# A block's maximum and its scaling in one instruction: products with minus the scale, their minimum accumulated

## The chip, the core and the metric

The kernel runs on one NeuronCore of a Trainium2 chip. The core has five engines with a queue each: TensorE (PE, matmuls), VectorE (DVE), ScalarE (ACT), GpSimd (POOL) and SyncE (SP, which here issues DMAs). Each works through its own queue in order and waits on semaphores for the others. The metric is the device time of one execution, in microseconds (us).

## What is computed

One layer of a streaming encoder on 512 tokens of width 1024 in float32: a modulated RMS norm and one input projection, then a convolution branch and an attention branch side by side, an output projection with a residual, and a mixture of experts. The change touches the attention alone, 8 heads, queries in blocks of 128:

```python
def block_attn(args):
    qb, blk = args
    sc = jnp.einsum("bqhd,bkhd->bhqk", qb, k).astype(jnp.float32) * scale
    q_chunk = (blk * Q_BLOCK + jnp.arange(Q_BLOCK)) // CHUNK
    mask = key_chunk[None, :] <= q_chunk[:, None]
    sc = jnp.where(mask[None, None], sc, -jnp.inf)
    p = jax.nn.softmax(sc, axis=-1).astype(v.dtype)
    return jnp.einsum("bhqk,bkhd->bqhd", p, v)
```

## The kernel before

The program is one long sequence, laid out by hand: in the stretch at issue PE, DVE, ACT and POOL each execute in the order in which the code names them (`manual_schedule`), so an instruction that waits holds up all that stands behind it on its engine.

*Before the attention,* `qkv_mm` makes queries, keys and values for one tile of 128 tokens at a time. Queries are not normalised; the norm's factor per token and head is kept in `qs` (128 tokens x 4 tiles x 8 heads), a root taken on POOL (`root`, L193) from the sums of squares. `qs_due` holds this root back: it is issued in the next tile's `qkv_mm`, behind the root of the keys, and at once for the last tile.

*The attention* is a loop over 32 blocks (L926): 8 heads with 4 query tiles each, head by head. Block i has 128 queries and (i mod 4 + 1) x 128 keys, so 128 to 512 columns. `scores` forms the products on PE in a PSUM bank (L867; the mask is in four further rows of queries and keys, a large negative number), DVE takes the maximum over the columns (L868) and multiplies it by minus the scale (L869, one column), and ACT computes exp(scale x product + bias) into an SBUF tile `e` with that bias and accumulates the row sums (L871). Two blocks later `p_tr` transposes `e` on PE (L881) and copies it out of PSUM, on DVE for the two narrow query tiles, on ACT for the wide ones (L882). After every two heads `attn_out` spreads the reciprocal sums by 16 matmuls (L891), multiplies by the values (L899) and DVE scales the result (L905), which ACT and POOL split in two parts (L670, L675).

*Beside it* run the convolution's matmuls (L334) and its layer norm (`conv_norm`: L693 on DVE, squares on ACT, sums on PE at L697), and `split_wout`: from block 7 on, a piece of the output weights is copied in a reduced format on DVE (the cast, L829) and the remainder is formed on POOL (the subtraction, L831), 12 pieces of 128x512 over the blocks 7 to 20, with each fifth block left free.

The tiles `e` come from a pool of 7 buffers of 128x512 (`T()`), the PSUM banks of the scores from one of 4 (`acc`), those of the transposes from one of 2 (`tr`).

Of the kernel before, what the change touches and what calls it, by code (L numbers as in the profile page):

```python
# [17 lines left out]
OP = mybir.AluOpType  # L18
AX = mybir.AxisListType
# [22 lines left out]
def hybrid_block(ctx: ExitStack, tc: tile.TileContext, A, out, dbg=None, stop=None):  # L42
    nc = tc.nc
    pe, act, dve, pool, sp = nc.tensor, nc.scalar, nc.vector, nc.gpsimd, nc.sync
# [42 lines left out]
    def nm(s):  # L87
        uid[0] += 1
        return f"{s}_{uid[0]}"
# [4 lines left out]
    def S(shape, dt=F32):  # L94
        return slots.tile(shape, dt, tag="s", name=nm("s"))

    def T(shape=(128, 512), dt=F32):
        return tmp.tile(list(shape), dt, tag="t", name=nm("t"))

    def small(w, dt=F32, bufs=4, tag=None):  # L100
        return tmp.tile([128, w], dt, tag=tag or f"sm{w}", name=nm("sm"), bufs=bufs)

    def acc(shape=(128, 512), dt=F32):
        return psum.tile(list(shape), dt, tag="acc", name=nm("acc"), bufs=4)
# [7 lines left out]
    def C(shape, dt=F32, name=None, uname=None):  # L112
        return const.tile(list(shape), dt, tag=name, name=uname or name)

    def mm3(o, lh, ll, rh, rl, start, stop):
        pe.matmul(o, lh, rh, start=start, stop=False)  # L116
        pe.matmul(o, lh, rl, start=False, stop=False)  # L117
        pe.matmul(o, ll, rh, start=False, stop=stop)  # L118
# [68 lines left out]
    def mean_eps(ssq, n, scale, eps=EPS):  # L187
        t = small(n, tag=f"rs{n}")
        dve.tensor_scalar(t, ssq, float(scale), eps, op0=OP.mult, op1=OP.add)
        return t  # L190

    def root(o, t, n):
        return pool.tensor_tensor(o, t, nhalf[:, :n], op=OP.pow)  # L193
# [84 lines left out]
    def run(g, n=100):  # L278
        for _ in range(n):
            if next(g, 0) == 0:  # L280
                break
# [69 lines left out]
    def tap(n):  # L351
        q = taps
        while n and q:
            if next(q[0], 0) == 0:
                q.pop(0)
            else:
                n -= 1
                if len(q) > 1:
                    q[0], q[1] = q[1], q[0]
# [156 lines left out]
    for tt in range(4):  # L516
        p = pcc[tt]
# [5 lines left out]
    for tt in range(4):  # L523
        p = pcc[tt]
# [7 lines left out]
    def rope_apply(o, src, TA, TB, nh):  # L532

        s4 = src.rearrange("p h (i d) -> p h i d", i=2)
        o4 = o.rearrange("p h (i d) -> p h i d", i=2)
        m = T()
        a1 = m[:, :nh * 32].rearrange("p (h i d) -> p h i d", h=nh, i=2)
        a2 = m[:, 256:256 + nh * 32].rearrange("p (h i d) -> p h i d", h=nh, i=2)
        pool.tensor_tensor(a1, s4, TA, op=OP.mult)
        for i in range(2):  # L540
            pool.tensor_tensor(a2[:, :, i, :], s4[:, :, 1 - i, :], TB[:, :, i, :], op=OP.mult)
        pool.tensor_tensor(o4, a1, a2, op=OP.add)
# [178 lines left out]

    ks = C([128, 4, 8], name="ks")
    qs = C([128, 4, 8], name="qs")
    vt = S([128, 4, 512])
    qT = [S([128, 4, 512]) for _ in range(2)]
    kT = [S([128, 4, 512]) for _ in range(2)]
# [14 lines left out]
    def qkv_mm(tt, g):  # L741
        cc = slice(tt * 128, (tt + 1) * 128)
        qktok = S([128, 2, 8, 96])
        qtok, ktok = qktok[:, 0], qktok[:, 1]
        pk = acc()
        wv = wkvs.rearrange("p s (h z d) -> p s h z d", z=2, d=64)
        mm3(pk, cTh[:, 2, cc], cTl[:, 2, cc], wv[:, 0, :, 0, :], wv[:, 1, :, 0, :], True, True)
        pk3 = pk.rearrange("p (h d) -> p h d", d=64)
        sq = T()
        act.activation(sq, pk, AF.Square)  # L750
        ssk = small(8, tag="ssk")
        tap(TK if tt < 3 else T3[0])
        dve.tensor_reduce(ssk, sq.rearrange("p (h d) -> p h d", d=64), axis=AX.X, op=OP.add)
        dve.tensor_scalar(ssk, ssk, cst[:, tt, 2:3], None, op0=OP.add)
        mk = mean_eps(ssk, 8, 1.0 / 96)
        ssq = small(8, tag="ssq")
        for hh in range(2):
            p = acc()
            for c in range(2):
                ns = slice(384 * hh, 384 * hh + 384)  # L760
                mm3(p[:, :384], cTh[:, c, cc], cTl[:, c, cc], wqh[:, c, ns], wql[:, c, ns], c == 0, c == 1)
            pq = p[:, :384].rearrange("p (h d) -> p h d", d=96)
            act.copy(qtok[:, 4 * hh:4 * hh + 4, :], pq)
            sq = T()
            act.activation(sq[:, :384], p[:, :384], AF.Square)
            run(g, 1)
            tap(TQ if tt < 3 else T3[1])
            dve.tensor_reduce(ssq[:, 4 * hh:4 * hh + 4], sq[:, :384].rearrange("p (h d) -> p h d", d=96), axis=AX.X, op=OP.add)
        rope_apply(qtok[:, :, 64:], qtok[:, :, 64:], *(t_[:, tt, None].to_broadcast([128, 8, 2, 16]) for t_ in rope["q"]), 8)
        root(ks[:, tt, :], mk, 8)  # L770
        for f in qs_due:
            f()
        qs_due.clear()
        dve.tensor_tensor(ktok[:, :, :64], pk3, ks[:, tt, :, None].to_broadcast([128, 8, 64]), op=OP.mult)  # L774
        kr = krr[:, tt]
        dve.tensor_tensor(ktok[:, :, 64:], kr[:, None, :].to_broadcast([128, 8, 32]),
                          ks[:, tt, :, None].to_broadcast([128, 8, 32]), op=OP.mult)

        mq = mean_eps(ssq, 8, 1.0, 96.0 * EPS)
        qs_due.append(lambda: root(qs[:, tt, :], mq, 8))  # L780
        if tt >= QS:
            qs_due.pop()()
        pvv = acc()
        mm3(pvv, cTh[:, 2, cc], cTl[:, 2, cc], wv[:, 0, :, 1, :], wv[:, 1, :, 1, :], True, True)
        act.copy(vt[:, tt, :], pvv)
        return qktok
# [15 lines left out]
    qs_due = []  # L802
    T3 = 0, 1, 4
    g = qkv_fill()
    tok = qkv_mm(0, g)
    for tt in range(4):
        nxt_ = qkv_mm(tt + 1, g) if tt < 3 else None
        if tt == REP_AT:
            load_rep(3)
        tap(PQ if tt < 3 else T3[2])  # L810
        if tt == 3:
            run(conv_steps, CM[0])
        for i, _ in enumerate(qkv_tr(tt, tok)):
            run(g, 1)
            if tt == 3 and i < 3:
                run(conv_steps, CM[i + 1])
        tok = nxt_
# [40 lines left out]
    heads = {}  # L858

    def scores(h, qt):  # L860
        hh, hi = h // 4, h % 4
        if qt == 0:
            heads[h] = dict(rs=small(4, tag="rsum"), mx=small(4, tag="mx"), nb=small(4, tag="nb"), e={})
        H = heads[h]
        n = (qt + 1) * 128
        p = acc()
        pe.matmul(p[:, :n], qT[hh][:100, hi, qt * 128:(qt + 1) * 128], kT[hh][:100, hi, :n], start=True, stop=True)  # L867
        dve.tensor_reduce(H["mx"][:, qt:qt + 1], p[:, :n], axis=AX.X, op=OP.max)  # L868
        dve.scalar_tensor_tensor(H["nb"][:, qt:qt + 1], H["mx"][:, qt:qt + 1], -1.0, qs[:, qt, h:h + 1], op0=OP.mult, op1=OP.mult)  # L869
        e = T()  # L870
        act.activation(e[:, :n], p[:, :n], AF.Exp, scale=qs[:, qt, h:h + 1], bias=H["nb"][:, qt:qt + 1],  # L871
                       accum_out=H["rs"][:, qt:qt + 1])
        H["e"][qt] = e
# [52 lines left out]
    for i in range(32 + LAG + 6):  # L926
        if i < 32:
            scores(i // 4, i % 4)
            tap(PT)
        k = i - LAG  # L930
        if 0 <= k < 32:
            p_tr(k // 4, k % 4)
        k -= 3
        if k >= 0 and k % 8 == 7:
            finish[k + 2] = attn_out(k // 8)
        if k in finish:
            finish.pop(k)()
        if i >= 7:
            run(splits, 1)
        if i in BG:  # L940
            run(bg, 1)
        if i >= 32:
            run(pre, PRE[i - 32])
        if i in NZ:
            run(norm, 1)
# [372 lines left out]
    for tt in range(4):  # L1318
        step = lambda k=1, tt=tt: run(rs_[tt], k)
        places = lambda tt=tt: (place(tt, 0, routed[tt][5]), tt < 3 and by_expert(tt, 0, routed[tt][5]))  # L1320
        n = 5 * tt + (5 if tt < 3 else 8)
        for d, f in ((0, lambda tt=tt: x2_part(tt, 0)), (D0, step), (D1, step)):
            at(n + d, f)
        if tt < 3:
            n = 31 + 8 * tt
# [382 lines left out]
```

## Time and profile before

| | us |
|---|---|
| median of 3 runs | 536.47 (535.53 to 536.54) |
| the profiled execution | 534.46 |
| its span, first to last instruction | 532.9 |
| PE busy in the span | 486.2 |
| DVE busy | 289.0 |
| ACT busy | 178.3 |
| POOL busy | 124.4 |
| the attention's blocks, from the first reduction to the last | 154.0 to 211.4 |

The rows below come from the one profiled execution, and times in them count from the start of its span. A row of the timeline gives start, duration, engine, line, operation, output <- inputs and shape; in square brackets stands how long the engine had been idle just before and which instruction ended that. Matmuls overlap in the pipeline, so durations of neighbouring ones do not add up. The granted clock is 1.00 where TensorE runs at 2.4 GHz and 0.50 where it runs at 1.2.

### The profile page before, as it was taken

The page shows a single profiled execution, that of the slowest core. Times are in us where ns is not written, and L with a number is a line of the kernel's source. Part 1 is how long each engine was busy: PE and PEld are TensorE (multiplying, and loading weights), DVE is VectorE, ACT ScalarE, POOL GpSimd, SP SyncE. Part 2 cuts the span into 40 slices and gives each one's busy share as a digit, 9 for nine tenths or more (in the row PEclk, how much of TensorE's full clock was granted, in tenths as well). Part 3 has the DMA queues.
Part 4 walks back from the last instruction along what each step waited for, and adds up shares of the span by engine and source line. Part 5 has one row for each costly group of instructions (what it writes and reads, how often), then busy time and mean ns, then how long its engine had stood idle before and what let it go on. Part 6 is the DMA issues. An engine that isn't in the chain of part 4 may idle for free.

```text
span 532.9 us, 8170 instructions
## 1 busy us (share of the span) xinstructions
PE 486.2 (91%) x2891; PEld 272.9 (51%) x2891; DVE 289.0 (54%) x655; ACT 178.3 (33%) x389; POOL 124.4 (23%) x118
## 2 busy tenths in 40 slices
PE   4899999999999898999998999999998999999982
PEld 4768975535644365788874343444433333223331
DVE  2447779957948675551556233436455454133544
ACT  4232744016575556821534422111201212021110
POOL 2311580007654543200000113012120212001100
PEclk9989999999999989999999999999999999999997
DMA  8999539985960262276968999999999999999934
GB/s 270 302 320 310 156 122 325 368 330 174 247 228 9 73 237 92 75 271 220 361 197 321 292 355 371 317 405 413 398 415 408 411 413 411 410 417 409 414 162 164
DMA packets 57859, 154.42 MB, mean 290 GB/s; under 512 B 7337, under 2 KB 26937, under 8 KB 51664
## 3 DMA queue, kind: packets, MB, share of 16 engines
q1 hardware_dynamic: 53232, 143.89, 75.6%
q10 hardware_dynamic: 2688, 5.92, 3.0%
q0 software_dynamic: 1888, 4.00, 2.3%
q8 instruction: 25, 0.41, 0.3%
q14 instruction: 26, 0.21, 0.1%
HBM read 150.97 MB, written 4.77 MB: 292 GB/s over the span
## 4 chain that ended last, share of the span: by engine, by line
PE 69%; DVE 13%; DMA 6%; ACT 4%; SPq 3%; issue 2%; POOL 1%; DVEq 0%; ACTq 0%; POOLq 0%
PE acc L1451 18%; PE acc L1477 9%; PE f L1495 8%; PE acc L116 5%; PE acc L118 4%; PE acc L117 4%; DVE s L1498 3%; DVE dw L346 2%; PE f L334 2%; DMA s<-in_w_ada_dram 2%; PE tr L1425 2%; DMA w<-in_w_ada_dram 2%; PE f L574 2%; PE acc L899 2%; DMA xg<-t 2%
## 5 line engine op out<-in xcount | busy, mean ns | idle before, releaser
L1451 PE MATMUL acc<-s,gw 128*32 128x512 f32 (+1 forms) x408 | 92.5, 597 | 0.0
L1498 DVE TENSOR_TENSOR s<-s,f 128x512 f32<-128x512 f32 x76 | 49.6, 685 | 35.9 <-PE f L1495 35.9
L116 PE MATMUL acc<-s,s 128*128 128x512 f32 (+3 forms) x160 | 63.2, 395 | 1.0 <-DVE s L774 1.0
L1495 PE MATMUL f<-s,t 128*128 128x512 f32 x184 | 54.4, 425 | 8.8 <-DVE s L1498 5.4
L118 PE MATMUL acc<-s,s 128*128 128x512 f32 (+3 forms) x160 | 58.8, 368 | 0.0
L117 PE MATMUL acc<-s,s 128*128 128x512 f32 (+3 forms) x160 | 58.8, 367 | 0.0
L346 DVE SCALAR_TENSOR_TENSOR dw<-s,cwh,dw 128x512 f32<-128x512 f32 x60 | 49.8, 844 | 1.2
L1451 PEld LDWEIGHTS acc<-s,gw 128*32 128x32 f32 (+1 forms) x408 | 24.6, 122 | 46.7 <-issue 44.8
L1451 PE MATMUL acc<-w,gw 128*32 128x512 f32 (+1 forms) x120 | 48.2, 622 | 0.0
L1482 POOL TENSOR_TENSOR s<-t,s 128x512 fp32r<-128x512 f32 x22 | 28.2, 1281 | 85.1 <-ACT s L1481 79.1
L1495 PEld LDWEIGHTS f<-s,t 128*128 128x128 f32 x184 | 30.0, 188 | 33.0 <-DVE s L1498 16.9
L1477 PE MATMUL acc<-s,t 128*64 128x512 f32 (+1 forms) x184 | 44.5, 598 | 0.0
L1454 ACT ACTIVATE t<-acc 128x256 f32<-128x256 f32 x12 | 4.6, 384 | 111.5 <-PE acc L1451 111.5
L116 PEld LDWEIGHTS acc<-s,s 128*128 128x128 f32 x160 | 30.2, 189 | 14.8 <-issue 7.9
L1456 DVE TENSOR_TENSOR t<-t,acc 128x256 f32<-128x256 f32 x12 | 5.1, 421 | 58.4 <-ACT t L1454 58.4
L1481 ACT CAST s<-t 128x512 fp32r<-128x512 f32 x24 | 14.8, 618 | 63.7 <-DVE t L1480 56.7
L1409 POOL DMA_INDIRECT s<-xg,sidx x11 | 11.7, 1060 | 98.1 <-PE tr L1425 61.7
L118 PEld LDWEIGHTS acc<-s,s 128*128 128x128 f32 x160 | 30.1, 188 | 4.1
L117 PEld LDWEIGHTS acc<-s,s 128*128 128x128 f32 x160 | 30.2, 189 | 3.3 <-issue 0.2
L1480 DVE SCALAR_TENSOR_TENSOR t<-acc,rt,gw 128x512 f32<-128x512 f32 x24 | 18.0, 750 | 25.0 <-PE acc L1477 25.0
L871 ACT ACTIVATE t<-acc,sm,qs 128x128 f32<-128x128 f32 (+3 forms) x32 | 19.7, 616 | 21.6 <-DVE sm L869 18.4
L868 DVE TENSOR_REDUCE sm<-acc 128x1 f32<-128x128 f32 (+3 forms) x32 | 15.5, 486 | 19.8 <-PE acc L867 19.7
(311 smaller groups left out, 817.1 us busy)
## 6 DMA issues: line engine op xcount, KB each, us to landing
s<-in_w_gate_e_dram SPq DMA_DIRECT2D x49, 512.0 KB
s<-in_w_up_e_dram SPq DMA_DIRECT2D x49, 512.0 KB, 10.9
s<-in_w_down_e_dram SPq DMA_DIRECT2D x22, 1024.0 KB, 12.5
w<-in_w_ada_dram SPq DMA_DIRECT2D x16, 1024.0 KB, 8.4
w<-in_w_down_e_dram SPq DMA_DIRECT2D x10, 1024.0 KB, 5.0
w<-in_w_gate_e_dram SPq DMA_DIRECT2D x15, 512.0 KB
w<-in_w_up_e_dram SPq DMA_DIRECT2D x15, 512.0 KB, 9.2
s<-in_w_ada_dram SPq DMA_DIRECT2D x6, 1024.0 KB, 11.2
```

The lines of the kernel that those rows point to most:

```text
L116: pe.matmul(o, lh, rh, start=start, stop=False)
L117: pe.matmul(o, lh, rl, start=False, stop=False)
L118: pe.matmul(o, ll, rh, start=False, stop=stop)
L346: dve.scalar_tensor_tensor(dw[:, t, :], u[:, t // 2, k:k + 512], w, dw[:, t, :], op0=OP.mult, op1=OP.add)
L868: dve.tensor_reduce(H["mx"][:, qt:qt + 1], p[:, :n], axis=AX.X, op=OP.max)
L871: act.activation(e[:, :n], p[:, :n], AF.Exp, scale=qs[:, qt, h:h + 1], bias=H["nb"][:, qt:qt + 1], accum_out=H["rs"][:, qt:qt + 1])
L1451: pe.matmul(gu[sl, :], self.hg[:, j, sl], w.t[:, :, j % 4, :], start=(j == 0), stop=(j == 7), tile_position=(0, o_), skip_group_check=True)
L1477: pe.matmul(o[o_:o_ + w_, :], self.aT[:, n * c + o_:n * c + o_ + w_], w.t[:, c, hs], start=(c == 0), stop=(c == 1), tile_position=(0, o_), ...
L1480: dve.scalar_tensor_tensor(yf[:n], o[:n], self.gate, gf[:n, hs], op0=OP.mult, op1=OP.mult)
L1482: eng.tensor_tensor(self.yhl[:n, 1, hs], yf[:n], self.yhl[:n, 0, hs].bitcast(F32), op=OP.subtract)
L1495: pe.matmul(o, u_.ot[:u_.n, tt * 128:(tt + 1) * 128], u_.yhl[:u_.n, k, 512 * hf:512 * hf + 512], start=(m == 0 and k == 0), stop=(m == len ...
L1498: dve.tensor_tensor(xr, xr, o, op=OP.add)
```

## The change

The reduction and the small product become one DVE instruction: every score is multiplied by minus the scale, the products are written to `e` (where ACT's exponential then overwrites them), and their minimum over the columns is accumulated. Since the scale is positive, this minimum is minus the scale times the maximum, the bias as before. Minus the scale is kept in a new tile `nqs`, made on POOL behind each root of `qs`. The tile `e` is now taken before the DVE instruction instead of after it, and the small tile `mx` is gone.

```diff
     qs = C([128, 4, 8], name="qs")
+    nqs = C([128, 4, 8], name="nqs")
...
-        qs_due.append(lambda: root(qs[:, tt, :], mq, 8))
+        qs_due.append(lambda: (root(qs[:, tt, :], mq, 8), pool.tensor_scalar(nqs[:, tt, :], qs[:, tt, :], -1.0, None, op0=OP.mult)))
...
-            heads[h] = dict(rs=small(4, tag="rsum"), mx=small(4, tag="mx"), nb=small(4, tag="nb"), e={})
+            heads[h] = dict(rs=small(4, tag="rsum"), nb=small(4, tag="nb"), e={})
...
-        dve.tensor_reduce(H["mx"][:, qt:qt + 1], p[:, :n], axis=AX.X, op=OP.max)
-        dve.scalar_tensor_tensor(H["nb"][:, qt:qt + 1], H["mx"][:, qt:qt + 1], -1.0, qs[:, qt, h:h + 1], op0=OP.mult, op1=OP.mult)
         e = T()
+
+        dve.tensor_scalar(e[:, :n], p[:, :n], nqs[:, qt, h:h + 1], None, op0=OP.mult, op1=OP.min, accum_out=H["nb"][:, qt:qt + 1])
```

On DVE, from the cast in block 7 to that in block 9, the queue stood like this before (the names `sm` are the small tiles of maxima and biases, `acc` the scores, `s` and `w` the output weights, `rec` the reciprocal sums):

```order
L829 CAST s_1538<-w_1303 128x512
L868 TENSOR_REDUCE sm_1546<-acc_1548 128x1
L869 SCALAR_TENSOR_TENSOR sm_1547<-sm_1546,qs 128x1
L829 CAST s_1538<-w_1303 128x512
L868 TENSOR_REDUCE sm_1546<-acc_1561 128x1
L869 SCALAR_TENSOR_TENSOR sm_1547<-sm_1546,qs 128x1
L885 RECIPROCAL rec<-sm_1487 128x4
```

and stands like this now, lines counted one to three higher:

```order
L830 CAST s_1533<-w_1306 128x512
L871 TENSOR_SCALAR t_1544,sm_1541<-acc_1542,nqs 128x128
L830 CAST s_1533<-w_1306 128x512
L871 TENSOR_SCALAR t_1556,sm_1541<-acc_1554,nqs 128x256
L886 RECIPROCAL rec<-sm_1487 128x4
```

Each pair has become one instruction with two outputs, `e` (a `t` tile) and the bias; the casts keep their places behind it.

On POOL, at the end of `qkv_mm` for the last tile, before:

```order
L193 TENSOR_TENSOR ks<-sm_1339,nhalf 128x8
L193 TENSOR_TENSOR qs<-sm_1274,nhalf 128x8
L193 TENSOR_TENSOR qs<-sm_1374,nhalf 128x8
L831 TENSOR_TENSOR s_1539<-w_1303,s_1538 128x512 x4
L831 TENSOR_TENSOR s_1645<-w_1327,s_1644 128x512
```

and now:

```order
L193 TENSOR_TENSOR ks<-sm_1342,nhalf 128x8
L193 TENSOR_TENSOR qs<-sm_1277,nhalf 128x8
L781 TENSOR_SCALAR nqs<-qs 128x8
L193 TENSOR_TENSOR qs<-sm_1378,nhalf 128x8
L781 TENSOR_SCALAR nqs<-qs 128x8
L832 TENSOR_TENSOR s_1534<-w_1306,s_1533 128x512 x4
L832 TENSOR_TENSOR s_1633<-w_1330,s_1632 128x512
```

A product stands behind each root of `qs`, and so ahead of the root of the last tile. The same holds for the two earlier tiles.

## Rows read from the trace of the kernel before

**Rows 1.** The page, busy share of the DMA engines in 40 slices of the span

```profile
DMA  8999539985960262276968999999999999999934
```

**Rows 2.** Busy time by stretch (columns as the first row names them)

```profile
core 0: us, PE busy (x) PEld busy (x) DVE busy (x) ACT busy (x) POOL busy (x), PEclk, DMA share, GB/s
180.00:187.00 7.00, 4.14 (x19) 2.00 (x17) 6.86 (x14) 3.96 (x11) 6.31 (x6) 1.00 0.07 9
188.00:192.00 4.00, 3.81 (x28) 3.04 (x28) 3.44 (x8) 2.27 (x7) 2.81 (x3) 0.57 0.52 182
210.00:214.00 4.00, 2.64 (x13) 1.22 (x12) 3.56 (x10) 3.28 (x10) 1.85 (x3) 1.00 0.54 207
```

**Rows 3.** Waits from 150 to 216 us: total, times, longest

```profile
ACT t L871 <- DVE sm L869: 18.4, 22, 2.5
```

**Rows 4.** Groups of DVE by form: busy us, mean ns, idle us before

```profile
L869 DVE SCALAR_TENSOR_TENSOR sm<-sm,qs 128x1 f32<-128x1 f32 x32 | 11.6, 364 | 1.2
L256 DVE TENSOR_SCALAR t<-tr,G,H 128x512 f32<-128x512 f32 x8 | 6.5, 809 | 3.1 <-ACT s L255 3.0
L829 DVE CAST s<-w 128x512 fp32r<-128x512 f32 x12 | 6.3, 522 | 0.0
L868 DVE TENSOR_REDUCE sm<-acc 128x1 f32<-128x512 f32 x8 | 5.5, 685 | 0.5 <-PE acc L867 0.4
```

**Rows 5.** Line 869 by itself: shortest, median and longest in ns

```profile
L869 DVE SCALAR_TENSOR_TENSOR sm<-sm,qs x32: 158/160/998, 154.3 to 212.2; 128x1 f32<-128x1 f32 x32
```

**Rows 6.** Timeline from 164.9 to 172.1 us, blocks 8 to 12

```profile
164.97 1.27 POOL L831 TENSOR_TENSOR s<-w,s 128x512 fp32r<-128x512 f32 x1 [11.15 <-DVE s L829]
164.97 0.29 DVE L868 TENSOR_REDUCE sm<-acc 128x1 f32<-128x128 f32 x1
...
165.30 0.96 DVE L869 SCALAR_TENSOR_TENSOR sm<-sm,qs 128x1 f32<-128x1 f32 x1
...
166.18 0.41 DVE L829 CAST s<-w 128x512 fp32r<-128x512 f32 x1
...
170.90 0.73 DVE L869 SCALAR_TENSOR_TENSOR sm<-sm,qs 128x1 f32<-128x1 f32 x1
...
172.02 1.09 PE L891 MATMUL tr<-ident,rec 128*64 128x128 f32 x16 [0.59 <-DVE s L882]
```

**Rows 7.** Timeline from 180 to 190 us, blocks 15 to 19

```profile
180.72 0.29 DVE L869 SCALAR_TENSOR_TENSOR sm<-sm,qs 128x1 f32<-128x1 f32 x1
...
188.41 0.73 DVE L869 SCALAR_TENSOR_TENSOR sm<-sm,qs 128x1 f32<-128x1 f32 x1
...
189.53 1.97 PE L891 MATMUL tr<-ident,rec 128*64 128x128 f32 x16 [0.20 <-DVE s L882]
```

**Rows 8.** Timeline from 198 to 214 us, blocks 23 and 31

```profile
198.61 0.62 DVE L869 SCALAR_TENSOR_TENSOR sm<-sm,qs 128x1 f32<-128x1 f32 x1
...
200.25 0.66 PE L881 MATMUL tr<-ident,t 128*128 128x128 f32 x4 [0.79 <-ACT t L871]
...
212.16 0.64 DVE L869 SCALAR_TENSOR_TENSOR sm<-sm,qs 128x1 f32<-128x1 f32 x1
...
213.57 1.04 POOL L193 TENSOR_TENSOR sm<-sm,nhalf 128x4 f32<-128x4 f32 x1
...
213.82 0.66 PE L881 MATMUL tr<-ident,t 128*128 128x128 f32 x4 [0.95 <-ACT t L871]
```

**Rows 9.** Timeline at 395 us, in the mixture of experts

```profile
395.15 1.27 POOL L1482 TENSOR_TENSOR s<-t,s 128x512 fp32r<-128x512 f32 x1 [7.91 <-ACT s L1481]
395.44 0.75 DVE L1480 SCALAR_TENSOR_TENSOR t<-acc,rt,gw 128x512 f32<-128x512 f32 x1 [1.02 <-PE acc L1477]
```

**Rows 10.** Timeline of DVE at 263 us, in the routing

```profile
262.89 0.18 DVE L1180 SCALAR_TENSOR_TENSOR sm<-Mall,tr 128x32 f32<-128x32 bf16 x1
262.99 0.08 DVE L1180 DVE_READ_ACCUMULATOR sm<-Mall,tr 128x1 f32 x1
```

**Rows 11.** Timeline, the last roots of the query scales, and block 3

```profile
150.58 3.24 POOL L193 TENSOR_TENSOR qs<-sm,nhalf 128x8 f32<-128x8 f32 x2
...
157.69 0.69 DVE L868 TENSOR_REDUCE sm<-acc 128x1 f32<-128x512 f32 x1 [0.44 <-PE acc L867]
```

## The prediction
> **What bounds the kernel now.** The page comes first: TensorE (PE) is busy for most of the span and the DMA engines are full from about 290 us on, empty around 160 to 215 us [rows 1]. That second hollow is the attention stage, where the changed lines run, so I looked at it alone. The list of waits there shows who waits for the instruction that the change removes: ScalarE (ACT) waited 18.4 us, 22 times, for the small product at L869 [rows 3]. The table of forms gives its price: 32 instructions, 11.6 us, a mean of 364 ns for one column [rows 4], although its shortest and its median are 158 and 160 ns and its longest 998 [rows 5]. So 11.6 - 32 x 0.16 = 6.5 us of it is not work. The timeline tells what it is: the product of block 8 (I count blocks in the order of issue, 0 to 31) starts at 165.30, while GpSimd (POOL) is inside a subtraction from 164.97 to 166.24, and ends at 166.26 [rows 6]. Twelve of the 32 are held like this (blocks 8 to 11, 15 to 20, 23, 31), each until a POOL instruction ends. The reduction just before, which reads PSUM, runs beside POOL at its plain 0.29 us [rows 6].
>
> The last thing to read is whether the holds lie on the path. From 180 to 187 us VectorE (DVE) is busy 6.86 of 7.00 us and PE only 4.14 [rows 2]: DVE leads there. PE's stalls name the same chain, for instance 0.79 and 0.95 us before the transposes of blocks 23 and 31, which wait for ACT's exponential, which waits for the held product [rows 8].
>
> **What the change does, and what it costs.**
>
> *The new instruction, unheld.* It reads PSUM, takes one scalar per partition from SBUF, and writes to SBUF. Nearest rows for 512 columns: the reduction takes 685 ns (one end), a tensor_scalar from PSUM with two such scalars 809 [rows 4] (the other). I take 0.75, an instruction with one such scalar and PSUM input [rows 9]. So about 0.065 more than the reduction, at every width. With an accumulator there is a second, short instruction: it takes 0.08 us, starts 0.10 after the main one and ends with it (262.89 + 0.18 and 262.99 + 0.08) [rows 10]. So the bias is ready d + 0.075 after the start, where d is the reduction's time; before, it took d + 0.04 (block 8: from 164.97 to the product at 165.30) + 0.16 = d + 0.20. ACT gains 0.125 us per block, DVE itself almost nothing: its next instruction could start d + 0.12 after the reduction's start and now can d + 0.095.
>
> The page "VectorE: DVE Perf Modes" of the Trainium skill, section "Rules for kernel authors", calls the reduction DVE's slowest operation and advises restructuring. The rows disagree: 685 ns for it and 0.75 us for what replaces it. By the rule, with an op as short as the reduction, 13 blocks on the path would give 13 x 0.065 = 0.8 us more, 532.0.
>
> *Does it escape the hold?* The nearest row is a product of PSUM data with one SBUF operand and one scalar: it starts at 395.44, inside a POOL subtraction of 395.15 to 396.42, and takes its plain 0.75 [rows 9]. I take no hold. But the cast at L829, SBUF to SBUF, is held too: 12 of them take 6.3 us [rows 4], and unheld, at 0.41 [rows 6], they would take 4.9; so 1.4 us is hold, all of it at blocks 15 and 17. It stands behind the product in DVE's queue in 12 blocks. So part of the hold only moves to the cast. I therefore walk through the stage, POOL's own work unchanged.
>
> The Trainium skill, page "SBUF — State Buffer", section "Who interferes with whom", says which DVE instructions share a port pair with GpSimd: casts that can use two ports, and those with two SBUF inputs; not a tensor_scalar that also writes out its accumulator. By that rule the product and the cast are held and the new instruction isn't, as in the rows.
>
> *Blocks 0 to 7:* PE works nearly without a gap; nothing gained. *Blocks 8 to 11:* the cast of block 8 waits for the same POOL instruction, so DVE goes on when it did before, and only the exponentials come earlier. The loop of cast and POOL subtraction (1.27 us) sets the pace for three blocks and gains 0.24 by its third turn. Block 11 has no cast behind it, so its hold (0.73 - 0.16 = 0.57 [rows 6]) goes whole. PE's wait at 172.02 [rows 6] ends **0.8 us** sooner. Next late there is PE itself.
>
> *Blocks 15 to 19:* five products are held, 0.13 the first and 0.57 the last [rows 7], 2.3 us in all, and casts 1.4: 3.7 us in an engine without idle time, up to the copy for which PE waits at 189.53 [rows 7]. POOL's queue holds three subtractions there and a fourth behind the cast of block 17, and after the change three casts still meet them. Counted with all of the stage 0.8 earlier: the cast of block 15 comes at 180.3 and waits until 180.9, when the work in front ends (0.57); three pieces of 1.27 us [rows 6], with the casts between them, then end near 182.35, 183.85 and 185.1; the cast of block 17 comes at 182.1 (0.26), that of block 18 at 184.1 (1.02). Together 1.85. 3.7 - 1.85 = 1.85, and 5 blocks at 0.025 of DVE make **2.0 us**.
>
> *Blocks 20 to 23:* the hold of block 23 (0.62 - 0.16 = 0.46) plus 0.125 brings its exponential forward by 0.59, inside PE's stall of 0.79 [rows 8]. The next stage, a square that waits for DVE, has gained 0.46, and 0.05 comes at block 26: **0.5 us**. *Blocks 29 to 31:* the hold of block 31 (0.64 - 0.16 = 0.48) plus 0.125 gives 0.6 of PE's 0.95. Of this I keep **0.4**: the next matmuls need a POOL root that starts at 213.57 behind the same POOL work [rows 8], and that hardly moves.
>
> *Added on POOL:* four products of 128x8, one behind each root of the query scales. The roots of the last two tiles end at 150.58 + 3.24 = 153.82; block 3, the first to need the last of them, starts at 157.69 [rows 11]. The form isn't in the trace; it costs more than nothing and no more than a root, 1.6. Even two at 1.6 end at 157.0, before block 3. I take 0; from 1.9 us each on, block 3 would wait. The wait for the buffer of the exponentials' output moves from ACT to DVE, where the casts and copies queue behind it; its last readers are transposes or POOL work of at least four blocks earlier, so 0.
>
> **Sum:** 0.8 + 2.0 + 0.5 + 0.4 = 3.7 us of the span of 532.9. After this stage PE is the path, and weights are fetched when PE's instructions free their buffers, so I let all of it through. The profiled execution took 534.46 and would take 530.8; the median of the runs, 2.0 higher, goes from 536.47 to **532.8**.
>
> *Left at zero:* PE's clock. After 180 to 187, with PE busy 4.14 of 7.00, the granted clock is 0.57 in 188 to 192 [rows 2], between the 1.2 and the 2.4 GHz level. Sixteen matmuls take 1.97 us there and 1.09 at 172.02 [rows 6, 7], and with those behind them some 1.1 us is lost on the path. With the shorter stalls PE would be busy about 4.4 of 6.2 us. In 210 to 214 it was busy 2.64 of 4.00 at clock 1.00 [rows 2], so the fall may go; one row doesn't show it, and the range has the 1.1.
>
> **Rivals.**
>
> *The hold moves whole to the casts.* Then only blocks without a cast behind them gain: 0.57 + 0.5 + 0.4 = 1.5 us, **535.0**. For it: the held casts [rows 4], and POOL's subtractions that start right behind each cast. Against it: block 16 has no cast behind it, and the casts' holds were already part of the 3.7.
>
> *The gain is absorbed by the weights.* The DMA engines are full from 290 to 506 us [rows 1]; if that stream ends when it ended before, nothing is gained: **536.5**. Against it: the stream has hollows before 290 (a 6 in the slice before), so it starts when buffers come free, which moves with PE.
>
> *The accumulation halves the rate (slower).* The reduction's slope is (685 - 290) / 384 = 1.03 ns per column [rows 4, 6]. One more clock per column adds 0.13, 0.26, 0.40 and 0.53 us to the four widths. Over the blocks on the path (8 to 11, 15 to 19, 23, 26, 30, 31) that is 5.1 us, so 5.1 - 3.7 = 1.4 slower, **537.9**. It decides from 0.73 clocks per column on. For it: no accumulation over hundreds of columns is in the trace. Against it: one over 32 columns takes 0.18 [rows 10], no mark of a second clock, though that would be only 0.03.
>
> *The new instruction is held too.* Then the reduction no longer runs under POOL's work: up to 0.29 to 0.69 lost in each of eleven blocks, some 4 us, **540**. Rows 9 speak against it.
>
> **How the numbers follow.** 0.2% is 1.1 us, about what a measurement tells here. Forecast 0.60; moved hold 0.20; absorbed 0.10; half rate 0.07; held 0.03. Faster by over 0.2%: the forecast and four fifths of the moved hold, 0.76. Slower: 0.09, from the last two. Within: 0.15. The range reaches down by the clock and another 0.9 (casts that meet POOL at luckier moments), to 530.8, and up to just short of the absorbed case, 536.4, leaving out the two slow cases and some of each tail.
>
> **What would show it.** L869 and its 11.6 us are gone; the new instruction takes 0.35, 0.48, 0.62 and 0.75 with a smallest spread beside POOL; casts hold longer in sum than their 1.4 us before; ACT's wait for DVE falls from 18.4 by at least 5; the 16 matmuls of 172.02 start 0.8 earlier, those of 189.53 2.8 earlier, and the stage ends 3.7 earlier. I am wrong if the new instruction takes a second clock per column or waits for POOL, or if the 3.7 seen at 215 us isn't there at 500.

## The result, and the profile of the changed kernel

The changed kernel took 526.95 us (median of 526.49, 529.35 and 526.95) against 536.47: a ratio of 0.9851, with a 95% interval of 0.9821 to 0.9882. Two further sets of runs, each beside the kernel before, gave 528.24 us (0.9844, 0.9814 to 0.9874) and 528.35 us (0.9878, 0.9851 to 0.9905). The prediction said 532.8 and at best 530.8: the sign was right, and so was the mechanism in part, but the size, 3.7 us, was less than half of what came.

The profiled execution of the changed kernel took 526.49 us, its span 524.9. Lines are one to three higher than before (scores L868, new instruction L871, exponential L872, cast L830, POOL's subtraction L832). Three stretches by engine, as in [rows 2]:

```profile
core 0: us, PE busy (x) PEld busy (x) DVE busy (x) ACT busy (x) POOL busy (x), PEclk, DMA share, GB/s
180.00:187.00 7.00, 5.91 (x44) 3.86 (x46) 7.00 (x20) 4.66 (x14) 7.00 (x6) 1.00 0.22 61
188.00:192.00 4.00, 4.00 (x29) 2.98 (x26) 1.68 (x5) 2.14 (x5) 1.71 (x2) 1.00 0.48 141
210.00:214.00 4.00, 4.00 (x32) 2.97 (x32) 1.94 (x4) 3.87 (x7) 0.00 (x0) 1.00 0.01 2
```

VectorE still leads from 180 to 187, but TensorE is now busy for 5.91 of those 7.00 us instead of 4.14, and the granted clock stays at 1.00 in 188 to 192, where it was 0.57. The same times hold somewhat later work here, as the changed kernel is 1.5 to 6.4 us ahead in them, and 210 to 214 lies behind its attention stage; the clock is 1.00 over that whole stage (rows in the next section).

The groups of VectorE by form, to be held against [rows 4] (busy us, mean ns, idle before):

```profile
L830 DVE CAST s<-w 128x512 fp32r<-128x512 f32 x12 | 9.1, 762 | 0.0
...
L871 DVE TENSOR_SCALAR_CACHE_REDUCE t<-acc,nqs 128x512 f32<-128x512 f32 x8 | 6.0, 744 | 0.9 <-issue 0.6
...
L871 DVE TENSOR_SCALAR_CACHE_REDUCE t<-acc,nqs 128x384 f32<-128x384 f32 x8 | 4.9, 616 | 7.6 <-PE acc L868 6.2 <-issue 1.4
...
L871 DVE TENSOR_SCALAR_CACHE_REDUCE t<-acc,nqs 128x256 f32<-128x256 f32 x8 | 3.8, 481 | 9.8 <-PE acc L868 9.7
...
L871 DVE TENSOR_SCALAR_CACHE_REDUCE t<-acc,nqs 128x128 f32<-128x128 f32 x8 | 2.8, 346 | 2.9 <-PE acc L868 2.9
...
L871 DVE DVE_READ_ACCUMULATOR t<-acc,nqs 128x1 f32 x32 | 2.6, 82 | 0.0
```

The same line by itself (shortest, median, longest in ns):

```profile
L871 DVE TENSOR_SCALAR_CACHE_REDUCE t<-acc,nqs x32: 339/546/751, 153.7 to 205.5; 128x128 f32<-128x128 f32 x8, 128x256 f32<-128x256 f32 x8, 128x384 f32<-128x384 f32 x8, 128x512 f32<-128x512 f32 x8
```

From the list of waits, ScalarE's wait for it (total, times, longest), which was 18.4 us [rows 3]:

```profile
ACT t L872 <- DVE t L871: 13.6, 17, 2.2
```

No fused instruction takes more than 751 ns, and in the timeline those of one width agree within 0.01 us, so none is held; the product's longest was 998 [rows 5]. The hold shows in the casts instead, 762 ns on average for 522 before. Block 8, in the timeline of the changed kernel, stands against [rows 6] (start, duration):

```profile
164.64 1.27 POOL L832 TENSOR_TENSOR s<-w,s 128x512 fp32r<-128x512 f32 x1 [10.40 <-DVE s L830]
...
164.76 0.35 DVE L871 TENSOR_SCALAR_CACHE_REDUCE t<-acc,nqs 128x128 f32<-128x128 f32 x1 [0.21 <-PE acc L868]
...
165.03 0.08 DVE L871 DVE_READ_ACCUMULATOR t<-acc,nqs 128x1 f32 x1
...
165.03 1.15 DVE L830 CAST s<-w 128x512 fp32r<-128x512 f32 x1
...
165.22 0.46 ACT L872 ACTIVATE t<-acc,sm,qs 128x128 f32<-128x128 f32 x1 [0.37 <-DVE t L871]
```

The fused instruction runs beside POOL's subtraction at its plain 0.35 us; the cast behind it is what is held now: it takes 1.15 us where it took 0.41 [rows 6], and ends 0.27 behind the subtraction (165.91). The exponential, which used to come after the hold, starts at 165.22.

Where the gain arises, read from the same landmarks in both traces (starts in us; "first scores" is the first score matmul, L707 the TensorE work behind block 31):

| landmark | before | changed | sooner by | new there |
|---|---|---|---|---|
| first scores | 153.53 | 153.31 | 0.22 | 0.2 |
| 16 matmuls behind block 11 | 172.02 | 170.63 | 1.39 | 1.2 |
| 16 matmuls behind block 19 | 189.53 | 185.58 | 3.95 | 2.6 |
| scores of block 21 | 193.71 | 188.75 | 4.96 | 1.0 |
| 16 matmuls behind block 27 | 204.97 | 199.18 | 5.79 | 0.8 |
| L707 | 215.01 | 208.61 | 6.40 | 0.6 |
| second expert unit | 302.15 | 294.09 | 8.06 | 1.7 |
| last expert unit | 506.17 | 498.14 | 8.03 | 0.0 |

So all of it is there at the last unit: nothing was absorbed downstream.

### The profile page after: what moved, and what is told of

It is laid out like the page before. It is cut to its first block, busy times and chain, and to the rows that moved or that the text cites. A ratio compares the mean times of both kernels' runs of the same rounds, so it can differ in the third digit from the quotient of the medians.

```text
span 524.9 us, 8174 instructions
## 1 busy us (share of the span) xinstructions
PE 481.2 (92%) x2891; PEld 271.1 (52%) x2891; DVE 282.2 (54%) x655; ACT 177.9 (34%) x389; POOL 125.9 (24%) x122
## 4 chain that ended last, share of the span: by engine, by line
PE 70%; DVE 10%; DMA 7%; SPq 4%; ACT 4%; issue 2%; POOL 1%; DVEq 0%; ACTq 0%; POOLq 0%
PE acc L1452 18%; PE acc L1478 9%; PE f L1496 8%; PE acc L116 5%; PE acc L118 4%; PE acc L117 4%; DVE s L1499 3%; PE f L334 3%; DMA s<-in_w_ada_dram 2%; SPq L167 2%; DVE dw L346 2%; PE acc L868 2%; PE tr L1426 2%; DMA w<-in_w_ada_dram 2%; PE f L574 2%
## 5 line engine op out<-in xcount | busy, mean ns | idle before, releaser
L1452 PE MATMUL acc<-w,gw 128*32 128x512 f32 (+1 forms) x120 | 46.8, 595 | 0.1
L871 DVE TENSOR_SCALAR_CACHE_REDUCE t<-acc,nqs 128x128 f32<-128x128 f32 (+3 forms) x32 | 17.4, 547 | 21.2 <-PE acc L868 18.8
L1478 PE MATMUL acc<-w,t 128*32 128x512 f32 (+1 forms) x80 | 26.0, 597 | 0.0
```

The lines of the kernel that those rows point to most:

```text
L871: dve.tensor_scalar(e[:, :n], p[:, :n], nqs[:, qt, h:h + 1], None, op0=OP.mult, op1=OP.min, accum_out=H["nb"][:, qt:qt + 1])
L1452: pe.matmul(gu[sl, :], self.hg[:, j, sl], w.t[:, :, j % 4, :], start=(j == 0), stop=(j == 7), tile_position=(0, o_), skip_group_check=True)
L1478: pe.matmul(o[o_:o_ + w_, :], self.aT[:, n * c + o_:n * c + o_ + w_], w.t[:, c, hs], start=(c == 0), stop=(c == 1), tile_position=(0, o_), ...
```

## The experiments

I call "the stage" the time from the first score matmul to L707. It is a steadier measure than the total: 55.3 us in each of five profiles of the changed kernel or of it with fillers placed behind the stage. One row of each of the two kernels shows the whole stage, busy time by engine (columns as above). Before:

```profile
153.53:215.01 61.48, 54.65 (x338) 31.32 (x337) 40.83 (x109) 38.25 (x98) 23.82 (x26) 0.97 0.38 123
```

Changed:

```profile
153.31:208.61 55.30, 52.77 (x339) 30.06 (x337) 34.32 (x109) 37.90 (x98) 24.99 (x27) 1.00 0.40 137
```

VectorE's 40.83 us of busy time, holds included, became 34.32. TensorE is now busy for 52.77 of 55.30, so another 2.5 us is the most that could be had from the stage by relieving the other engines.

**First: is it the hold?** The changed kernel once more, beside three kernels.

> The changed kernel again, beside the three others of this call. If the clock's falls are a part of the gain that comes and goes from execution to execution, single times scatter by 1 to 3 us and the longer ones show the lower granted clock; the median stays near 527. If the whole gain is fixed work, the times agree within 1 us.

528.24 us; stage 55.29. The six times spread over 3.6 us, and the three shorter ones have granted clocks of 0.990 to 0.995, the three longer ones 0.986 or 0.987: the first branch. (Later in this section the changed kernel is run a third time, and there the order does not hold: 527.52 us at 0.987, 530.36 at 0.990.)

> The kernel before, with the small product as a tensor_scalar: the maximum times the scale as a per-partition scalar, times -1. It has one SBUF tensor input instead of two; reduction and product stay two instructions, nothing is fused. Theory A, the gain is the product's wait for POOL: most of it comes, 528 to 530, and the product's longest time falls from 998 ns to under 250. Theory B, the gain comes from the fused instruction itself (a shorter chain to the bias, one instruction fewer): 535 to 537. If a tensor_scalar of one column from SBUF to SBUF is held too, its times show it and the time is that of theory B for another reason.

```diff
-        dve.scalar_tensor_tensor(H["nb"][:, qt:qt + 1], H["mx"][:, qt:qt + 1], -1.0, qs[:, qt, h:h + 1], op0=OP.mult, op1=OP.mult)
+        dve.tensor_scalar(H["nb"][:, qt:qt + 1], H["mx"][:, qt:qt + 1], qs[:, qt, h:h + 1], -1.0, op0=OP.mult, op1=OP.mult)
```

531.9 us, ratio 0.9913 (0.9885 to 0.9942): half of the gain, between the two theories. Its product by itself, in ns:

```profile
L869 DVE TENSOR_SCALAR sm<-sm,qs x32: 213/214/216, 154.7 to 208.2; 128x1 f32<-128x1 f32 x32
```

and its casts in the table of groups:

```profile
L829 DVE CAST s<-w 128x512 fp32r<-128x512 f32 x12 | 7.9, 659 | 0.0
```

The product's hold is gone without any fusion, and the stage fell by 4.7 us, to 56.74, with the clock at 1.00 (columns as above):

```profile
153.97:210.71 56.74, 52.94 (x339) 30.04 (x337) 37.72 (x109) 38.01 (x98) 24.55 (x26) 1.00 0.40 133
```

The fusion takes off another 1.4.

> The changed kernel, with a product of two SBUF operands put back behind the accumulated minimum (times 1 and a column of ones), whose result is the bias. The fused instruction stays. Theory A: the holds are back and the fused instruction is 0.065 us longer than the reduction was, so the time is that of the kernel before or up to 1 us more, 535.5 to 538. Theory B: one small instruction of 0.16 us more per block, 13 of the blocks on the path, 529 to 530.

```diff
-            heads[h] = dict(rs=small(4, tag="rsum"), nb=small(4, tag="nb"), e={})
+            heads[h] = dict(rs=small(4, tag="rsum"), mx=small(4, tag="mx"), nb=small(4, tag="nb"), e={})
...
-        dve.tensor_scalar(e[:, :n], p[:, :n], nqs[:, qt, h:h + 1], None, op0=OP.mult, op1=OP.min, accum_out=H["nb"][:, qt:qt + 1])
+        dve.tensor_scalar(e[:, :n], p[:, :n], nqs[:, qt, h:h + 1], None, op0=OP.mult, op1=OP.min, accum_out=H["mx"][:, qt:qt + 1])
+        dve.scalar_tensor_tensor(H["nb"][:, qt:qt + 1], H["mx"][:, qt:qt + 1], 1.0, ones[:, :1], op0=OP.mult, op1=OP.mult)
```

535.85 us (0.9977, 0.9954 to 1.0), stage 62.03: the gain is gone. The products are held again and the casts are back at 523 ns:

```profile
L872 DVE SCALAR_TENSOR_TENSOR sm<-sm,ones 128x1 f32<-128x1 f32 x32 | 10.9, 340 | 1.1
...
L830 DVE CAST s<-w 128x512 fp32r<-128x512 f32 x12 | 6.3, 523 | 0.0
```

> The kernel before, with the score matmuls of blocks 17 to 19 issued twice into the same bank, in the stretch in which PE waits for DVE. The chain through DVE is unchanged. If PE's stalls there cause the fall of its clock at 188 to 192 us: the clock stays at 1.00, the 16 matmuls behind take 1.1 instead of 1.97 us and the time falls by about 1 us. If the fall has another cause: no change, or up to 1 us slower by the doubled matmuls.

```diff
         pe.matmul(p[:, :n], qT[hh][:100, hi, qt * 128:(qt + 1) * 128], kT[hh][:100, hi, :n], start=True, stop=True)
+        if 17 <= 4 * h + qt <= 19:
+            pe.matmul(p[:, :n], qT[hh][:100, hi, qt * 128:(qt + 1) * 128], kT[hh][:100, hi, :n], start=True, stop=True)
```

534.88 us (0.9963, 0.9944 to 0.9983). Its 16 matmuls behind block 19 (L893 here) take 1.09 us instead of the 1.97 of [rows 7], at a granted clock of 1.00 over the stage, and the stage is 60.48, 1.0 us shorter:

```profile
153.96:214.44 60.48, 54.87 (x344) 31.28 (x343) 40.83 (x109) 38.25 (x98) 23.83 (x26) 1.00 0.37 124
```

That is the price of the fall of the clock there, and the changed kernel, in which TensorE has fewer gaps ahead, does not pay it.

**Second: hold or VectorE's load?** The twelve casts go to ScalarE in three kernels, by one edit:

```diff
-    HI, LO, HI1, LO1 = dve.tensor_copy, pool, act.copy, dve
+    HI, LO, HI1, LO1 = act.copy, pool, act.copy, dve
```

> The changed kernel with the twelve 128x512 casts moved from VectorE to ScalarE. In the changed kernel they are held (762 ns on average, 9.1 us in all), and in its attention stage TensorE is busy for 52.8 of 55.3 us, so no more than 2.5 us can be had. Theory A (the hold left the product and what is left of it sits in the casts, partly on the path): the stage becomes 1 to 2 us shorter, 526 to 527.5 us against 528.2 for the changed kernel. Theory B (ScalarE pays instead: twelve copies of about 0.58 us, 7 us more on an engine that is busy for 37.9 of those 55.3 us, and the exponentials queue behind them): 529 to 531. Theory C (the casts' hold lies beside TensorE's work): within 0.5 us of the changed kernel.

529.4 us (0.988, 0.9857 to 0.9902); stage 55.17. Its stage by engine:

```profile
154.05:209.22 55.17, 52.69 (x339) 30.04 (x337) 26.75 (x97) 43.38 (x110) 24.09 (x27) 1.00 0.40 136
```

The stage speaks for theory C: with the held casts gone from VectorE it is 0.1 us shorter. That is a net figure: what ScalarE's 5.5 us more (43.38 for 37.90) cost, this run does not separate. The total lies in theory B's span all the same; the intervals of the two ratios overlap, so I read nothing from it but that this version is not better than the changed kernel.

> The kernel before with the twelve casts moved to ScalarE; the maximum's reduction and the product stay as they were. Tells whether the held product or VectorE's total load was the price. Theory A (the product is held beside GpSimd's loop, wherever the casts are): products still take about 360 ns on average, the stage from its first score matmul to the matmul after it stays above 59 us (61.5 before, 55.3 changed), time 533 to 536.5. Theory B (VectorE was simply too full: 40.8 us busy of 61.5, and 6.3 us of casts gone serve as well as a fusion): products fall to about 160 to 250 ns and the time to 527 to 530.

531.8 us (0.9921, 0.9894 to 0.9949). Neither theory: the products are still held, 321 ns on average, and yet the stage is 56.88, 4.6 us shorter than before. Its stage by engine:

```profile
155.76:212.64 56.88, 52.66 (x339) 30.16 (x337) 34.48 (x97) 43.87 (x110) 23.66 (x26) 1.00 0.39 133
```

and its product in the table of groups:

```profile
L869 DVE SCALAR_TENSOR_TENSOR sm<-sm,qs 128x1 f32<-128x1 f32 x32 | 10.3, 321 | 1.2
```

> The kernel with separate reduction and product, the product with one SBUF tensor input (213 ns, never held in the earlier run), and the twelve casts on ScalarE. Nothing held is left on VectorE here, nor in the changed kernel with its casts on ScalarE, so the difference of these two is the fusion alone: for 512 columns 685 plus 213 ns against 744. Theory A (the shorter chain from scores to exponential is worth something by itself; with the casts on VectorE it was 1.4 us of stage): 1 to 2 us slower than that kernel. Theory C (the fusion is worth nothing without the hold): the same within 0.5 us.

This joins the product of one SBUF tensor input with the casts on ScalarE. 531.52 us (0.9933, 0.9907 to 0.9959); stage 56.12, 0.95 longer than the changed kernel with its casts on ScalarE:

```profile
154.20:210.32 56.12, 52.77 (x338) 30.02 (x336) 31.40 (x97) 43.45 (x110) 23.59 (x26) 1.00 0.41 135
```

With nothing held and VectorE far from full (31.4 and 26.8 us), that is what the fusion is worth as a shorter way alone: theory A, just under its 1 to 2 in the stage and just over it in the medians (2.1).

These stages also show what a hold costs where VectorE is not full. With the casts on ScalarE, exchanging the held product for the one that is never held takes 0.76 us off the stage (56.88 to 56.12); with the casts on VectorE the same exchange took off 4.7, of which the clock is 1.0.

> The changed kernel with nine matmuls of 128x128 (about 0.136 us each) into unused columns, placed in the 1.5 us in which TensorE waits for VectorE ahead of the first expert unit; their result is used by nothing. In one profiled execution of the changed kernel the granted clock fell to 0.5 for some 4 us after that wait, in another it did not, and before the change it fell too. Theory A (the fall follows that idle stretch, and it is a part of the gain that comes and goes between executions): the clock stays at 1.00 through the first expert unit, whose first 16 matmuls take 3.7 us and the eight transposes ahead of them 1.1; median 0.5 to 1.3 us below the changed kernel's 528.2, lowest run unchanged. Theory B (the fall has nothing to do with that wait, or fillers push the path): same median, or up to 1 us slower.

```diff
     def order_out():
+        for _ in range(9):
+            pe.matmul(plt[0][:, 0], ident, ident, start=False, stop=True, skip_group_check=True)
```

(with `plt` made `[128, 4, 128]` and its logits in the first 40 columns of each.) 529.79 us (0.989, 0.987 to 0.991). The first 16 matmuls of the first expert unit took 3.72 us, at full clock, but each filler showed as two matmuls, and together they took 2.27 us, so they pushed the way by 0.64. No gain.

**Third: on the way, or anywhere?** An added product that is not held, behind the fused instruction, once with nobody waiting for it and once on the way.

> The changed kernel once more, beside the three kernels of this call. Its attention stage (from the first score matmul to the transposes after its last block) took 55.3 us in each of three profiles, with or without fillers elsewhere: 55.2 to 55.4 again. The whole should be 527 to 529.5 us, as the granted clock falls in some executions and not in others at two places outside the stage.

528.35 us (0.9878, 0.9851 to 0.9905); stage 55.28.

> The changed kernel with a product of one SBUF tensor input (about 0.21 us, not held) behind each of the 32 fused instructions; nothing uses its result, so the exponential need not wait for it, and 6.8 us are added to VectorE's queue. Theory A (what a block pays is what stands between its scores and its exponential): the stage is 55.3 to 55.9 us, no more than 0.6 longer than the changed kernel's. Theory B (VectorE's total time in the stage is what is paid, wherever it stands): 56.3 to 57.5.

```diff
+        dve.tensor_scalar(small(1, tag="jk1", bufs=2), H["nb"][:, qt:qt + 1], ones[:, :1], 1.0, op0=OP.mult, op1=OP.mult)
```

533.15 us (0.9962, 0.9935 to 0.9988), stage 60.25: far from theory A, and beyond B.

```profile
153.73:213.98 60.25, 54.58 (x338) 31.05 (x336) 40.74 (x141) 38.31 (x98) 24.57 (x27) 0.97 0.39 125
```

> The changed kernel with the same product of one SBUF tensor input, now on the way: the fused instruction's minimum goes through it before the exponential takes it. It is the twin of the kernel with the held product put back, whose stage took 62.0 us. Theory A (the hold is the larger part): stage 56.6 to 57.6, so 1.3 to 2.3 us for the longer way and 4.4 to 5.4 for the hold and the fall of the clock that goes with it. Rival (any second instruction on the way costs about as much, held or not): 60 to 62.

(the edit of the held product above, with `dve.tensor_scalar(..., ones[:, :1], 1.0, op0=OP.mult, op1=OP.mult)` in its place.) 531.81 us (0.9931, 0.9899 to 0.9964), stage 58.68: between the two.

```profile
153.96:212.64 58.68, 52.94 (x339) 29.95 (x337) 40.81 (x141) 38.27 (x98) 24.60 (x27) 1.00 0.38 128
```

The landmarks of the two twins, off the way first:

```profile
171.43 1.09 PE L893 MATMUL tr<-ident,rec 128*64 128x128 f32 x16 [0.31 <-DVE s L884]
...
188.08 1.87 PE L893 MATMUL tr<-ident,rec 128*64 128x128 f32 x16 [0.91 <-DVE s L884]
```

and on the way:

```profile
171.76 1.09 PE L893 MATMUL tr<-ident,rec 128*64 128x128 f32 x16 [0.32 <-DVE s L884]
...
188.42 1.09 PE L893 MATMUL tr<-ident,rec 128*64 128x128 f32 x16 [0.92 <-DVE s L884]
```

Counted from their first scores (153.73 and 153.96) these are 17.70 and 34.35 us, and 17.80 and 34.46. So up to there it makes 0.1 us of difference whether the exponential waits for the product or not. What they pay alike is 6.8 us more in VectorE's queue. The 1.6 us by which the first is longer in the end comes behind 188 us, where its clock fell (1.87 against 1.09) and its twin's did not. From 181 to 188 us TensorE was busy for 4.49 of 7.00 us in both, so its stalls ahead do not by themselves decide whether the clock falls; what does, no run here shows.

> The changed kernel with five filler matmuls instead of nine in the 1.5 us ahead of the first expert unit in which TensorE waits for VectorE: each showed as two passes of 0.126 us, so five take 1.26 us and fit, where nine took 2.27 and pushed the path by 0.64. Theory A (the fall of the clock at the first expert unit follows that wait and costs 1.1 to 1.8 us in the executions that have it): its first 16 matmuls take 3.7 us and the median is 0.5 to 1.3 below the changed kernel's of this call. Theory B (that fall is replaced by one elsewhere, or comes all the same): within 0.5 us of it.

528.4 us against 528.35: theory B. The wait was filled and the first unit ran at full clock (3.72 us), but a transfer held the next one up by 0.70, and the total stayed.

**Fourth: the rest of the median.** Three more profiles of the kernel before, one execution each.

> The kernel before, profiled again. In three comparisons the medians differ by 7.7 to 9.5 us, but the stage by only 6.2 in the profiles, and the profiled execution of the kernel before was among its fastest (534.5 of 533.3 to 539.8). Theory A: the stage takes 61.3 to 61.7 us in every execution, and what the median has on top are falls of the granted clock outside the stage, which the changed kernel has less often by chance. Theory B: the stage itself takes longer in other executions, 62 to 63.5 us, with the clock at its lower level for longer or in a second place, so the change takes away more than 6.2.

> As for the profile before this one: theory A 61.3 to 61.7 us of stage, theory B 62 to 63.5 in some of the three.

> As for the two before this one: theory A 61.3 to 61.7 us of stage, theory B 62 to 63.5 in some of the three.

Stages of 61.65, 61.32 and 62.14 us: with the first one, four of them between 61.3 and 62.1, each with a mean clock of 0.97. In all four the 16 matmuls behind block 19 are slow (1.97, 1.98, 1.50 and 1.98 us; 1.09 in every profile of the changed kernel). Two of the three lie in theory A's span, the last just in B's. The whole took 541.82, 535.21 and 537.12 us, and the rest of that spread lies outside the stage: in the second of these executions, for one, the first unit's 16 matmuls took 4.69 us, in the third 3.72.

## Why the prediction missed

**Right, by its steps.** The new instruction takes 0.35, 0.48, 0.62 and 0.74 us, where 0.35, 0.48, 0.62 and 0.75 were forecast; that leaves no room for a second clock per column, and it is not held. The hold moves in part to the casts: in blocks 15 to 19 they waited 1.9 us (0.96, 0.73, 1.39 and 0.48 less 0.41 each), forecast 1.85; that the stage paid this much for them is not shown, since moving every cast to ScalarE brought the 16 matmuls behind block 19 only 0.2 us sooner (32.07 us after the first scores for 32.27). POOL's four products take 0.24 to 0.26 us and delay nothing. All that the stage gains reaches the end. ScalarE's wait fell by 4.8, just short of the "at least 5". Two readings of [rows 1] were loose, and the sum does not rest on them: the hollow of 160 to 215 us is not empty (0, 2, 6 and 2 tenths), and the 6 ahead of the full stretch stands two slices before it, not one. The Trainium skill, page "SBUF — State Buffer", section "Who interferes with whom", says that a DVE instruction with two SBUF inputs, and a cast that can use two ports, contend with GpSimd for a shared port pair, while a tensor_scalar that writes out its accumulator does not enter such a two-port mode; the rows here agree, with longest durations of 998 ns for the product [rows 5], casts of up to 1.39 us, and 751 ns for the fused instruction.

**The step that failed: "DVE itself almost nothing".** I wrote that VectorE's next instruction could start d + 0.12 after the reduction's start and now can d + 0.095, 0.025 us sooner per block. The second figure puts it behind the fused instruction's end (d + 0.065); it starts ahead of that end. A block of 384 columns in the timeline of before:

```profile
178.21 0.56 DVE L868 TENSOR_REDUCE sm<-acc 128x1 f32<-128x384 f32 x1 [1.26 <-PE acc L867]
...
178.80 0.16 DVE L869 SCALAR_TENSOR_TENSOR sm<-sm,qs 128x1 f32<-128x1 f32 x1
...
178.87 0.28 DVE L882 COPY s<-tr 128x128 f32<-128x128 f32 x1
```

and the same block in the changed kernel:

```profile
176.82 0.62 DVE L871 TENSOR_SCALAR_CACHE_REDUCE t<-acc,nqs 128x384 f32<-128x384 f32 x1 [1.38 <-PE acc L868]
...
177.36 0.08 DVE L871 DVE_READ_ACCUMULATOR t<-acc,nqs 128x1 f32 x1
...
177.36 0.28 DVE L883 COPY s<-tr 128x128 f32<-128x128 f32 x1
...
177.54 0.67 ACT L872 ACTIVATE t<-acc,sm,qs 128x384 f32<-128x384 f32 x1 [0.78 <-DVE t L871]
```

The copy starts 0.66 us after the first instruction before, and 0.54 after it now: the reading of the accumulator and the next instruction both begin 0.08 us before the fused one ends. It is so at every width: in blocks that nothing holds, from block 5 on, the next instruction started 0.39, 0.53, 0.66 and 0.80 us after the first one's start before, and 0.27, 0.41, 0.54 and 0.67 now. VectorE gains 0.12 per block, 0.095 more than I allowed. Put into the sum, that alone mends the terms: blocks 8 to 11, 0.8 + 4 x 0.095 = 1.2 (measured 1.2); 15 to 19, 2.0 + 0.5 = 2.5 (2.6); 20 to 23, 0.5 + 0.4 = 0.9 (0.8). With 0.6 for the last blocks, for which I had 0.4, the stage without the clock gives 5.2, not 3.7. That is arithmetic after the result; the experiments bear it out. With the product's hold gone but nothing fused, the stage was 4.7 us shorter, 1.0 of it the clock: the remaining 3.7 are my whole sum. The fusion behind it, which I had put at almost nothing for VectorE, took off another 1.4, some of it because the product used there, at 0.21 us, is 0.05 longer than an unheld one before. (For the exponential the forecast of 0.125 per block holds: its start moved from 0.84 after the first instruction's start to 0.72.)

**Behind it: what is paid for.** I argued from the way from scores to exponential. The twins show that time added to VectorE's queue is paid alike on that way and off it. In one order, from the stage of before: 61.48; without the fall of the clock 60.48; with the same 40.8 us on VectorE but no held product 58.68; with 6.5 us less on VectorE 55.30. So the clock is about 1.0, the place of the hold 1.8, and plain VectorE time 3.4 of the 6.2 us. The split depends on the order in which one takes things away. With the product exchanged first (61.48, 56.74, 55.30) it is clock 1.0, hold 3.7 and fusion 1.4; with the casts gone from VectorE the hold is worth 0.8 and the fusion 0.95. Nor does VectorE's busy time alone set the stage: 34.48 us of it, with held products and the casts on ScalarE, went with 56.88 us, and the changed kernel's 34.32 with 55.30.

**The clock, left at zero,** was worth 1.0 in the stage, close to the 1.1 that I had worked out and kept for the range. The mean clock there is 0.97 in all four profiles of the kernel before and 1.00 in all three of the changed one, so it was a term of the sum and not the edge of the range. With both terms the stage's 6.2 us would have made the median 530.3, already below the 530.8 at which the range ended.

**What stays open.** The stage gives 6.2 us (6.4 from the mean of four profiles before), the medians 7.7 to 9.5. The rest lies outside the stage, where the clock falls in some executions of either kernel. The first expert unit's 16 matmuls show it; in the profiled execution of the changed kernel and in its third set of runs they read

```profile
284.39 3.72 PE L1452 MATMUL acc<-w,gw 128*64 128x512 f32 x16
```

```profile
284.51 5.37 PE L1452 MATMUL acc<-w,gw 128*64 128x512 f32 x16
```

The way from L707 to the second unit took 85.5 us in the first and 87.1 in the second of these, and in the first profile of before 87.14. In the last profile of before, where the unit had no fall, it took 85.42:

```profile
291.80 3.72 PE L1451 MATMUL acc<-w,gw 128*64 128x512 f32 x16
```

So the 1.7 us in the last-but-one row of the table above comes and goes with the clock in either kernel. That the earlier end of the stage makes such falls rarer is not shown. It may be more than chance: taking the stages off the medians (61.65, the mean of four, for the kernel before) leaves an estimated 471.7 to 473.1 us for the changed kernel in its three sets of runs and 474.1 to 474.8 for the kernel before in four. But the changed kernel with its casts on ScalarE leaves 474.2, so this does not go with the fused instruction as such, and its cause stays open.

**The rivals.** The moved hold came true only in part: the casts' holds rose from 1.4 us to 4.2, and taking the casts off VectorE was worth 0.1 us of stage, net of ScalarE's extra work. Absorption by the weights, the half rate and a hold of the new instruction did not occur.

## What to carry to other kernels

Where an engine is busy without a gap, price a fusion by the start of the next instruction on that engine, not only by the start of whoever waits for the result: an off-the-way instruction of 0.21 us cost this stage as much as one on the way, up to the point at which the clocks parted. A clock that falls right behind a stretch of stalls belongs into the sum of a change that shortens the stalls, with a chance, since in the twins equally busy stretches came once with the fall and once without. And measure between two landmarks in the trace: the changed kernel's stage repeated within 0.1 us where its totals spread over 3.9 (526.49 to 530.36); that of the kernel before, with its fall of the clock, spread over 0.8 in four profiles.

## What was not expected of the hardware

Reading the accumulator (82 ns) costs VectorE no time of its own here: it begins 0.08 us before its instruction ends, and so does the instruction behind it. A product of one column with one SBUF tensor input and one scalar per partition takes 212 to 216 ns in the four kernels that have it, longer than the 158 ns of the two-input form when that is not held, and it was never held. A hold is no fixed price: exchanging the held product for this one was worth 3.7 us of stage without the clock, with the casts in the same queue, and 0.8 with the casts on ScalarE.
